# A decoder layer on one core: weight-block sums and the down products' sums into x made by accumulating transfers

## The chip, the cores and the metric

The kernel runs on one core of a Trainium2 chip. The metric is the device time of one execution in microseconds (us); lower is better. Three runs of the kernel before took 1016.21, 1017.39 and 1019.45 us.

The engines go by the names that the profile uses: PE multiplies matrices (PEld is its weight loading), DVE is the vector engine, ACT the scalar engine, POOL is GpSimd, SP issues most of the transfers. PSUM is the memory into which PE writes (8 banks); SBUF is the memory from which all engines read.

## What is computed

One layer of a decoder for 512 prompt tokens and 8 sample tokens (520 columns in all), with shared weights, and a final norm. What matters here is its last part, the feed-forward network:

```python
h2 = rms_norm(x, norm2_g) * (1.0 + sc2) + sh2
gu, up = jnp.split(h2 @ w_ffn_in, 2, axis=-1)
x = x + g2 * ((jax.nn.silu(gu) * up) @ w_ffn_out)
...
y = rms_norm(x, normf_g)
```

The model width is 1024, the inner width 2816, all in float32. Before it stand the input projections, a recurrent branch, attention over the prompt, attention of the 8 sample tokens over cached pages, and the projections that join them.

## The kernel before, in words

Activations lie transposed: `x` is eight tiles of 128 features by 520 columns. Every float32 operand is split into a high part and a low part of the matmul type (float32r); a product is three matmuls for each 128 rows of the inner dimension (high·high, low·high, high·low), with 260 columns at a time, half of the 520. The splits of weights are made just ahead of their use: ACT copies the source into the high half of a tile `wb`, and DVE subtracts that from the source to get the low half (`split_four`, L267 to L272). There are six `wb` buffers, so a split can run at most six units of weights ahead of PE.

The feed-forward part works through 22 tiles of 128 inner features. A tile needs two blocks of columns of `w_ffn_in` (gate and up), which SP loads with two transfers of 512 KB into one of two `wraw` buffers (`load_chunks`, L201). The tiles 0 to 3 are plain. The tiles 4 to 21 are made by `fast_tile` (L1658), which does the 2x2 block product with seven block products in place of eight (a scheme of Strassen and Winograd). The weight blocks are A11, A12 (gate, upper and lower half of the inner dimension) and A21, A22 (up), and four sums of them, S1 to S4. `split_block` (L255) makes the four sums on POOL, into two tiles `ws`, when the tile's first block is split: S1 = A21 + A22, S2 = S1 - A11, S3 = A11 - A21, S4 = A12 - S2. The matching sums of the activations are made once (`h2_blocks`, L1634). The seven products run in the order of `BLOCKS`: A11, S2, S3, S1, A12, A22, S4, 12 matmuls each, into four banks X, Y, W, Z; the banks are summed into each other between products (L1676 to L1692). Two orders matter below: the product A22 adds onto bank W, so it may start when DVE has made Y from W (L1685), and that needs ACT's copy of bank Z (L1683).

Between these products stand the down products, which multiply finished groups of four inner tiles with `w_ffn_out` (24 matmuls each, PE line L307, tile `fo`): in the tiles 4 to 16 one behind S2 and one behind A12, in 17 to 20 only the one behind A12, in 21 both. So 32 down products lie in the fast tiles. Each ends in `residual` (L1468), which adds gate times product into `x` with four DVE instructions: one multiply-add for the first half (L1470), and for the second half a small product of the 8 sample columns (L1475), a multiply-add (L1476) and a small sum (L1478). The last six inner tiles are multiplied at the end (`last_product`, L1563), which also does the final norm.

The order of each engine's queue is set by the program's order and a scheduler; each engine works its queue in order, and an instruction that waits holds everything behind it. SP's load of the tile c+2 waits until all that read the `wraw` buffer of tile c is done.

Of the kernel before, what the change touches and what calls it, by code (L numbers as in the profile page):

```python
# [8 lines left out]
F32 = mybir.dt.float32  # L9
F32R = mybir.dt.float32r  # L10
I32 = mybir.dt.int32
AF = mybir.ActivationFunctionType
ALU = mybir.AluOpType
# [5 lines left out]
NP = 512  # L19
# [5 lines left out]
KT = 8  # L25
# [3 lines left out]
HALF = NT // 2  # L29
HALVES = ((0, HALF), (HALF, NT))  # L30
# [35 lines left out]
def kernel(ctx, tc, xT, par, gates, b_f, cst, cse, own, cache_k, cache_v, cache_lf, pt,  # L66
# [3 lines left out]
    pe, act, dve, pool, sp = nc.tensor, nc.scalar, nc.vector, nc.gpsimd, nc.sync  # L70
# [4 lines left out]
    pgp = ctx.enter_context(tc.tile_pool(name="pgp", bufs=7))  # L75
# [4 lines left out]
    def slot(name, cols=NT, dt=F32, parts=128):  # L80
        return heap.tile([parts, cols], dt, name=name, tag="slot")
# [12 lines left out]
    x = []  # L94
# [19 lines left out]
    mod = keep.tile([128, 6, KT, 9], F32, name="mod")  # L114
# [25 lines left out]
    GROUP = 4  # L140
# [14 lines left out]

    for c in range(len(chunks)):
        whole(c)
    joined = set()
    for jt in range(FF // 128):
        c = len(chunks)  # L160
        chunks.append(cols(w_fi, 128 * jt, 128) + cols(w_fi, FF + 128 * jt, 128))
        if jt < GROUP:
            whole(c)
            continue
        for name in BLOCKS:
            units.append((c, name, 4))
            if name in JOIN[jt]:
                g, i = JOIN[jt][name]
                if i % 2 == 0:
                    joined.add(len(chunks))  # L170
                    chunks.append(cols(w_fo, 128 * i, 256, 128 * GROUP * g, GROUP))
                units.append((max(joined), 128 * (i % 2), GROUP))
# [7 lines left out]
    raws, splits = {}, {}  # L180
# [20 lines left out]
    def load_chunks(upto):  # L201
        while state["dma"] < len(chunks) and state["dma"] <= upto:
            c = state["dma"]
            if c in joined:
                raw = pgp.tile([128, GROUP, 256], F32, name="wraw", tag="pg")
            else:
                raw = wp.tile([128, KT, 256], F32, name="wraw", tag="wraw", bufs=2)
            o = 0
            for src, r0, nk, c0, n in chunks[c]:
                sp.dma_start(raw[:, :nk, o:o + n],  # L210
                             src[r0:r0 + nk * 128, c0:c0 + n].rearrange("(k p) c -> p k c", p=128))
                o += n
            raws[c] = raw
            state["dma"] += 1
# [7 lines left out]
    def split_upto(n):  # L222
        while state["split"] < len(units) and state["split"] <= n:
            m = state["split"]
            c, o, nk = units[m]
            load_chunks(c)
            raw = raws[c]
            state["split"] += 1
            if isinstance(o, str):
                splits[m] = split_block(raw, o)  # L230
                continue
            if c in joined:
                splits[m] = split_four(raw[:, :, o:o + 128])
                continue
            his, los = [], []
            step = 4 if m in in_heap else KT
            for k0 in range(0, nk, step):
                k1 = min(nk, k0 + step)
                if m in in_heap:
                    hi = slot("whs", 512, F32R).rearrange("p (k c) -> p k c", c=128)  # L240
                    lo = slot("wls", 512, F32R).rearrange("p (k c) -> p k c", c=128)
                else:
                    hi = wp.tile([128, KT, 128], F32R, name="whi", tag="whi", bufs=3)
                    lo = wp.tile([128, KT, 128], F32R, name="wlo", tag="wlo", bufs=3)
                src = raw[:, k0:k1, o:o + 128]
                state["act"] = act.copy(hi[:, :k1 - k0], src)  # L246
                with held(m):
                    state["last"] = dve.tensor_tensor(lo[:, :k1 - k0], src, hi[:, :k1 - k0].bitcast(F32), ALU.subtract)  # L248
                his += [hi[:, k] for k in range(k1 - k0)]
                los += [lo[:, k] for k in range(k1 - k0)]  # L250
            splits[m] = (his, los)

    blocks = {}

    def split_block(raw, name):  # L255
        if name == "A11":
            a11, a12, a21, a22 = (raw[:, k:k + 4, o:o + 128] for o in (0, 128) for k in (0, 4))
            s12, s34 = (pgp.tile([128, 8, 128], F32, name="ws", tag="pg") for _ in range(2))
            s1, s2, s3, s4 = s12[:, :4], s12[:, 4:], s34[:, :4], s34[:, 4:]
            blocks.update(A11=a11, A12=a12, A22=a22, S1=s1, S2=s2, S3=s3, S4=s4)  # L260
            pool.tensor_tensor(s1, a21, a22, ALU.add)  # L261
            pool.tensor_tensor(s2, s1, a11, ALU.subtract)
            pool.tensor_tensor(s3, a11, a21, ALU.subtract)
            pool.tensor_tensor(s4, a12, s2, ALU.subtract)
        return split_four(blocks[name])

    def split_four(src):  # L267
        state["tag"] = "wlo" if state.get("tag") == "whi" else "whi"
        t = wp.tile([128, KT, 128], F32R, name="wb", tag=state["tag"], bufs=3)
        state["act"] = act.copy(t[:, :4], src)  # L270
        state["last"] = dve.tensor_tensor(t[:, 4:], src, t[:, :4].bitcast(F32), ALU.subtract)  # L271
        return [t[:, k] for k in range(4)], [t[:, 4 + k] for k in range(4)]  # L272
# [49 lines left out]
    def product(name, a, evac, mid=None, inside=None):  # L322
        n = begin()
        for j in range(2):
            b = bank(f"{name}_{j}")
            half_product(n, j, a, b, None if j else inside)
            evac(j, b[:, :HALF])
            if j == 0 and mid is not None:
                mid()
        run_later(n)  # L330
# [1303 lines left out]
    def h2_blocks(k):  # L1634
        b1, b2 = h2raw[k], h2raw[k + 4]
        u, w = slot("u"), slot("w")
        with tc.issue_after(state["blocks"].ins) if k != 3 else nullcontext():
            first = pool.tensor_tensor(w[:, R_], b2[:, R_], b1[:, R_], ALU.subtract)
        if k == 3:
            state["blocks"] = first  # L1640
        with tc.issue_after(state["blocks"].ins):
            pool.tensor_tensor(u[:, L_], b1[:, R_], b1[:, L_], ALU.subtract)
            pool.tensor_tensor(w[:, L_], b2[:, R_], u[:, L_], ALU.subtract)
            pool.tensor_tensor(u[:, R_], b2[:, L_], w[:, L_], ALU.subtract)
        traw[k] = u, w

    def split_blocks(k0):
# [10 lines left out]
    def fast_tile(jt, ac):  # L1658
        sw, cp, u2, out = slot("sw"), slot("cp"), slot("u2", HALF), pair_out()
        X, Y, W, Z = (bank(f"fi{jt}{n}")[:, :HALF] for n in "xywz")  # L1660
        into = {"A11": X, "S2": Y, "S3": W, "S1": Z, "A12": X, "A22": W, "S4": Z}
        add = lambda o_, a_, b_: dve.tensor_tensor(o_, b_, a_, ALU.add)

        def close(b, part):
            dve.tensor_tensor(b, b, sw[:, part], ALU.mult)
            split_part(out, b, part)

        for m_, name in enumerate(BLOCKS):
            n = begin()
            hi, lo = splits[n]  # L1670
            for k in range(4):
                ah, al = h2_block(name, k)
                for m, (wt, at) in enumerate(((hi, ah), (lo, ah), (hi, al))):
                    state["mm"] = pe.matmul(into[name], lhsT=wt[k], rhs=at, start=m_ < 4 and k == 0 and m == 0,
                                            stop=k == 3 and m == 2, skip_group_check=m_ > 3)
            if name == "A11":  # L1676
                act.copy(cp[:, L_], X)
            elif name == "S2":
                add(u2, cp[:, L_], Y)
            elif name == "S3":  # L1680
                add(W, u2, W)
            elif name == "S1":
                act.copy(cp[:, R_], Z)  # L1683
                add(Z, u2, Z)
                add(Y, cp[:, R_], W)  # L1685
            elif name == "A12":
                act.activation(sw[:, L_], X, AF.Silu)
            elif name == "A22":
                close(W, L_)
            elif name == "S4":  # L1690
                act.activation(sw[:, R_], Z, AF.Silu)
                close(Y, R_)  # L1692
            run_later(n)
            if name in JOIN[jt]:
                g, i = JOIN[jt][name]
                product(f"fo{g}_{i}", ac[GROUP * g:GROUP * g + GROUP], lambda j, b_, i=i: residual(i, b_, 5, j))
        return out

    ac, ts, ready = [], [slot("sw") for _ in range(PLAIN)], []
    u = state["n"]  # L1700
    for j in range(2):
# [92 lines left out]
```

## Time and profile before

| | |
|---|---|
| runs | 1016.21, 1017.39, 1019.45 us; median 1017.39 |
| span of the profiled execution | 1016.4 us (1.0 below the median of the runs; its own time is recorded only as this span) |
| PE busy | 994.3 us, 98% of the span |
| DVE / ACT / POOL busy | 797.3 / 547.5 / 327.6 us |
| the fast tiles, 700 to 980 us | PE 280.00 of 280.00 us, DVE 233.91, ACT 133.05, POOL 97.04, granted clock 1.00, DMA share 0.34 |
| from 980 us to the end | PE 27.31 of 36.40 us |

How to read it: the columns of the windows view are stretch, length, busy time of each engine with its count of instructions, granted clock of PE, share of the DMA engines, GB/s. In the timeline a row is start, length, engine, line, operation, out<-in, and, in brackets, how long the engine stood idle before and what ended that. "us to landing" is the time from the start of a transfer's issue to the arrival of its last byte's signal.

### The profile page before, as it was taken

What the parts mean: (1) busy time and instruction counts of PE and PEld (TensorE: products, weight loads), DVE (VectorE), ACT (ScalarE), POOL (GpSimd) and SP (SyncE); (2) the same over time, 40 slices, a digit from 0 to 9 for tenths busy, and PEclk for the clock granted to TensorE, in tenths of its full rate; (3) what the DMA queues carried; (4) which work ended last, traced back from release to release, by engine and by line L of the source; (5) the groups of instructions that cost most, each with busy time, mean ns of one, the idle gap of its engine ahead of it and who ended that gap; (6) DMA issues with size and microseconds to landing.
All of it is one profiled execution on the core that took longest, in us unless ns stands there. A gap on an engine that the chain in (4) does not pass through costs nothing.

```text
span 1016.4 us, 21281 instructions
## 1 busy us (share of the span) xinstructions
PE 994.3 (98%) x8012; PEld 921.1 (91%) x8012; DVE 797.3 (78%) x1423; ACT 547.5 (54%) x1128; POOL 327.6 (32%) x415
## 2 busy tenths in 40 slices
PE   5999999999999999999999999999999999999996
PEld 2799999999998988888888888999999999999996
DVE  5559999998999888886655544869988888888764
ACT  4534576848761576777783233554444444445553
POOL 0346111121143245653400001583442442425112
PEclk9999999999999999999999999999999999999998
DMA  9798857788879998995867995324234243233122
GB/s 325 250 324 279 242 189 202 243 261 278 281 250 345 331 312 286 321 294 190 251 216 269 319 340 186 84 74 115 81 108 125 63 125 98 70 104 105 63 64 85
DMA packets 164378, 206.97 MB, mean 204 GB/s; under 512 B 9827, under 2 KB 125043, under 8 KB 164211
## 3 DMA queue, kind: packets, MB, share of 16 engines
q1 hardware_dynamic: 147634, 152.78, 48.1%
q0 software_dynamic: 12960, 46.41, 13.8%
q10 hardware_dynamic: 3680, 6.42, 1.7%
q8 instruction: 63, 1.03, 0.4%
q14 instruction: 41, 0.33, 0.1%
HBM read 192.49 MB, written 13.09 MB: 202 GB/s over the span
## 4 chain that ended last, share of the span: by engine, by line
PE 93%; DMA 2%; DVE 2%; ACT 1%; issue 0%; SPq 0%; POOL 0%; DVEq 0%; POOLq 0%; ACTq 0%
PE fo L307 12%; PE k L307 5%; PE wo L307 5%; PE gb L307 5%; PE gr L307 5%; PE v L307 5%; PE ga L307 5%; PE xr L307 5%; PE pb L307 4%; PE pv L839 3%; PE pa L307 3%; PE po L1302 2%; PE qp L542 2%; PE q L542 2%; PE ada L374 2%; PE ptt L1268 2%
## 5 line engine op out<-in xcount | busy, mean ns | idle before, releaser
L246 ACT CAST whi<-wraw 128x1024 fp32r<-128x1024 f32 (+1 forms) x79 | 82.0, 1039 | 113.6 <-PE pb L307 34.3
L248 DVE TENSOR_TENSOR wlo<-wraw,whi 128x1024 fp32r<-128x1024 f32 (+1 forms) x79 | 99.1, 1256 | 19.0 <-ACT whi L246 16.6
L307 PE MATMUL fo<-ach,wb 128*128 128x260 f32 x512 | 93.4, 283 | 0.0
L270 ACT CAST wb<-ws 128x512 fp32r<-128x512 f32 x72 | 44.7, 621 | 86.0 <-PE fo L307 58.9
L700 POOL DMA_DIRECT2D pg<-in_cache_k_dram x74 | 39.6, 536 | 143.1 <-DVE S L751 62.6
L271 DVE TENSOR_TENSOR wb<-wraw,wb 128x512 fp32r<-128x512 f32 x86 | 76.4, 889 | 4.7 <-ACT wb L270 3.9
L307 PEld LDWEIGHTS fo<-ach,wb 128*128 128x128 f32 x512 | 78.9, 188 | 0.0
L271 DVE TENSOR_TENSOR wb<-ws,wb 128x512 fp32r<-128x512 f32 x72 | 68.7, 954 | 12.6 <-ACT wb L270 11.0
L261 POOL TENSOR_TENSOR ws<-wraw 128x512 f32<-128x512 f32 x18 | 24.4, 1353 | 153.2 <-DMA wraw<-in_w_fi_dram 104.1
L307 PE MATMUL fo<-acl,wb 128*128 128x260 f32 x256 | 72.2, 282 | 0.0
L270 ACT CAST wb<-wraw 128x512 fp32r<-128x512 f32 x86 | 53.5, 622 | 31.4 <-ACT cp L1683 6.2
L750 DVE TENSOR_TENSOR pg<-pg,qb 128x1024 f32<-128x1024 f32 x48 | 57.9, 1221 | 2.5 <-DMA pg<-in_cache_k_dram 2.5
L751 DVE TENSOR_REDUCE S<-pg 128x16 f32<-128x1024 f32 x48 | 57.4, 1209 | 0.2
L1259 POOL TENSOR_SCALAR p<-p,mu 128x128 f32<-128x128 f32 (+3 forms) x28 | 38.4, 1381 | 53.0 <-DVE mu L1255 47.1
L307 PEld LDWEIGHTS fo<-acl,wb 128*128 128x128 f32 x256 | 48.2, 188 | 0.0
L1253 ACT ACTIVATE p<-p,mu 128x128 f32<-128x128 f32 (+3 forms) x64 | 35.4, 554 | 18.2 <-DVE mu L1252 18.0
L307 PE MATMUL v<-hh,whi 128*128 128x260 f32 x128 | 38.2, 298 | 0.8 <-ACT row L819 0.5
L307 PE MATMUL k<-hh,whi 128*128 128x260 f32 x128 | 37.3, 292 | 0.0
L307 PE MATMUL pb<-oh,whi 128*128 128x260 f32 x128 | 37.1, 290 | 0.2 <-ACT oh L1360 0.2
L307 PE MATMUL gb<-hh,whi 128*128 128x260 f32 x128 | 37.0, 289 | 0.0
L307 PE MATMUL v<-hl,whi 128*128 128x260 f32 x128 | 36.9, 288 | 0.0
L307 PE MATMUL v<-hh,wlo 128*128 128x260 f32 x128 | 36.9, 288 | 0.0
(1101 smaller groups left out, 3957.3 us busy)
## 6 DMA issues: line engine op xcount, KB each, us to landing
araw<-in_ada_w_dram SPq DMA_DIRECT2D x48, 512.0 KB, 7.6
wraw<-in_w_fi_dram SPq DMA_DIRECT2D x44, 512.0 KB, 5.3
pg<-in_cache_k_dram POOLq DMA_DIRECT2D x42, 512.0 KB, 6.2
pg<-in_cache_v_dram SPq DMA_DIRECT2D x42, 512.0 KB, 5.5
wraw<-in_w_in_dram SPq DMA_DIRECT2D x34, 512.0 KB, 6.4
wraw<-in_w_in_dram SPq DMA_DIRECT2D x11, 1024.0 KB, 8.5
pg<-in_cache_v_dram POOLq DMA_DIRECT2D x22, 512.0 KB, 6.1
pg<-in_cache_k_dram POOLq DMA_DIRECT2D x32, 256.0 KB, 5.9
```

What stands on the lines that cost most here:

```text
L246: state["act"] = act.copy(hi[:, :k1 - k0], src)
L248: state["last"] = dve.tensor_tensor(lo[:, :k1 - k0], src, hi[:, :k1 - k0].bitcast(F32), ALU.subtract)
L270: state["act"] = act.copy(t[:, :4], src)
L271: state["last"] = dve.tensor_tensor(t[:, 4:], src, t[:, :4].bitcast(F32), ALU.subtract)
L307: state["mm"] = pe.matmul(out[:, :t1 - t0], lhsT=wt[k], rhs=at, start=k == 0 and m == 0, stop=k == nk - 1 and m == 2)
L542: state["mm"] = pe.matmul(b[:, :HALF], lhsT=wt, rhs=at[:, t0:t1], start=k == 0 and m == 0, stop=k == 3 and m == 2)
L700: done.append(eng.dma_start(pg, cache[bass.ds(r, 1), :, c0:c1].rearrange("a p c -> (a p) c")))
L750: dve.tensor_tensor(pg, pg, q, ALU.mult)
L751: last = dve.tensor_reduce(S[r // 2][:, c:c + H], pg.rearrange("p (h d) -> p h d", d=DH), AX.X, ALU.add)
L839: pe.matmul(pv[0][32 * gq:32 * gq + 32, :], lhsT=pw[r][:, c:c + 32], rhs=pgs[gq // 2][:, 512 * hf:512 * hf + 512], start=j == 0, stop=j == ...
L1253: act.activation(p[:, :n + 128], p[:, :n + 128], AF.Exp, bias=mu[:, 0:1], scale=-1.0, accum_out=mu[:, 1:2])
L1259: (pool.tensor_scalar(p, p, mu[:, 2:3], None, ALU.mult) if a and i + 1 < KT else act.activation(p, p, AF.Copy, scale=mu[:, 2:3]))
```

## The change

- Of the four weight sums POOL still makes S1, and now S2 = S1 + A11. S3 is made in place: a transfer issued by POOL adds A11 onto A21 in the `wraw` buffer. S4 is also made in place: a second transfer adds S2 onto A12, when A12 itself has been split. The signs of the activations' sums and of two sums of banks are turned to match.
- The two halves of `wraw` now lie one behind the other, so that each block is one run of 2 KB in a partition.
- One tile `ws` a fast tile in place of two. `block_sums` of the next tile stands in the program behind the split of A12.
- A down product no longer goes to `residual`: ACT multiplies its two halves by the gate into a tile `dn`, DVE multiplies the 8 sample columns, and a transfer issued by POOL adds the 128x520 tile `dn` onto `x`.
- `load=28` lets the program's text reach further ahead with loads in this part.

```diff
+                if c in fast:
+                    raw = raw.rearrange("p k c -> p (k c)").rearrange("p (o k c) -> p o k c", o=2, k=KT)
...
-            pool.tensor_tensor(s1, a21, a22, ALU.add)
-            pool.tensor_tensor(s2, s1, a11, ALU.subtract)
-            pool.tensor_tensor(s3, a11, a21, ALU.subtract)
-            pool.tensor_tensor(s4, a12, s2, ALU.subtract)
-        return split_four(blocks[name])
+    def block_sums(c):
+        load_chunks(c)
+        raw = raws[c]
+        a11, a12, a21, a22 = (raw[:, o, k:k + 4] for o in range(2) for k in (0, 4))
+        s12 = pgp.tile([128, 8, 128], F32, name="ws", tag="pg")
+        s1, s2 = s12[:, :4], s12[:, 4:]
+        blocks[c] = dict(A11=a11, A12=a12, A22=a22, S1=s1, S2=s2, S3=a21, S4=a12)
+        pool.tensor_tensor(s1, a21, a22, ALU.add)
+        pool.dma_start(a21, a11, accum_op=ALU.add)
+        pool.tensor_tensor(s2, s1, a11, ALU.add)
+
+    def split_block(c, name):
+        if c not in blocks:
+            block_sums(c)
+        pair = split_four(blocks[c][name])
+        if name == "A12":
+            pool.dma_start(blocks[c]["S4"], blocks[c]["S2"], accum_op=ALU.add)
+            for d in sorted(fast):
+                if d > c:
+                    block_sums(d)
+                    break
+        return pair
...
-                product(f"fo{g}_{i}", ac[GROUP * g:GROUP * g + GROUP], lambda j, b_, i=i: residual(i, b_, 5, j))
+                product(f"fo{g}_{i}", ac[GROUP * g:GROUP * g + GROUP], lambda j, b_, i=i: add_down(i, b_, j))
...
+    def add_down(f, ps, j):
+        t0, t1 = HALVES[j]
+        e_, gate = min(t1, NP), mod[:, 5, f]
+        if j == 0:
+            downs[f] = slot("dn")
+        t = downs[f]
+        act.activation(t[:, t0:e_], ps[:, :e_ - t0], AF.Copy, scale=gate[:, 0:1])
+        if j:
+            dve.tensor_tensor(t[:, NP:], ps[:, e_ - t0:HALF], gate[:, 1:9], ALU.mult)
+            pool.dma_start(x[f], downs.pop(f), accum_op=ALU.add)
+
+    state.update(load=28)
```

The orders of PE and of SP are the same in both programs. Two places on other engines change. Lines of the changed program are higher (by 4 at the weight sums, by 14 around the fast tiles).

POOL's queue in the fast tiles before; `wraw_10599` and `wraw_10806` are the buffers of the tiles 7 and 8, `ws` their sums:

```order
L261 TENSOR_TENSOR ws_10735<-wraw_10599 128x512
L263 TENSOR_TENSOR ws_10736<-wraw_10599 128x512
L262 TENSOR_TENSOR ws_10735<-ws_10735,wraw_10599 128x512
L264 TENSOR_TENSOR ws_10736<-wraw_10599,ws_10735 128x512
L261 TENSOR_TENSOR ws_10942<-wraw_10806 128x512
L263 TENSOR_TENSOR ws_10943<-wraw_10806 128x512
L262 TENSOR_TENSOR ws_10942<-ws_10942,wraw_10806 128x512
L264 TENSOR_TENSOR ws_10943<-wraw_10806,ws_10942 128x512
```

The same place now; the buffers of the tiles 6, 7 and 8 are `wraw_10321`, `wraw_10527` and `wraw_10733`, and a row with DMA is a transfer that adds:

```order
L274 DMA wraw_10321<-ws_10451 128x512
L1724 DMA x_8824<-dn_10755 128x520
L265 TENSOR_TENSOR ws_10863<-wraw_10733 128x512
L266 DMA wraw_10733<-wraw_10733 128x512
L267 TENSOR_TENSOR ws_10863<-ws_10863,wraw_10733 128x512
L1724 DMA x_8826<-dn_10841 128x520
L274 DMA wraw_10527<-ws_10657 128x512
L1724 DMA x_8828<-dn_10961 128x520
```

Where four sums of one tile stood in a row, the S4 transfer of a tile (L274; tile 7 in the last row but one) now stands behind the sums of the tile after it (tile 8) and behind the sum into `x` of a down product of the tile before (`dn_10841`, tile 6).

ACT's queue around the split of S4 of tile 7 before (`ws_10736` holds S4, `wraw_10806` is tile 8):

```order
L1677 COPY cp_10899<-fi7x_10903 128x260
L270 CAST wb_10923<-wraw_10599 128x512
L270 CAST wb_10939<-ws_10736 128x512
L270 CAST wb_10948<-wraw_10806 128x512
L270 CAST wb_10982<-ws_10942 128x512
L1683 COPY cp_10899<-fi7z_10906 128x260
```

And now (`wb_10942<-wraw_10527` is the split of S4, which the transfer made in the `wraw` buffer of tile 7):

```order
L1691 COPY cp_10899<-fi7x_10903 128x260
L284 CAST wb_10923<-wraw_10527 128x512
L1721 ACTIVATE dn_10961<-fo0_6_0_10948,mod_102 128x260
L284 CAST wb_10942<-wraw_10527 128x512
L1721 ACTIVATE dn_10961<-fo0_6_1_10963,mod_102 128x252
L284 CAST wb_10945<-wraw_10733 128x512
L284 CAST wb_10979<-ws_10863 128x512
L1697 COPY cp_10899<-fi7z_10906 128x260
```

The split of S4 reads the `wraw` buffer, and the two halves of the down product behind S2 (`dn_10961`) stand around it.

More of the change, by code (lines that the diff above doesn't have):

```diff
@@ L157 @@
         whole(c)
-    joined = set()
+    joined, fast = set(), set()
     for jt in range(FF // 128):
@@ L164 @@
             continue
+        fast.add(c)
         for name in BLOCKS:
@@ L207, in load_chunks @@
                 raw = wp.tile([128, KT, 256], F32, name="wraw", tag="wraw", bufs=2)
+                if c in fast:
+                    raw = raw.rearrange("p k c -> p (k c)").rearrange("p (o k c) -> p o k c", o=2, k=KT)
             o = 0
             for src, r0, nk, c0, n in chunks[c]:
-                sp.dma_start(raw[:, :nk, o:o + n],
+                sp.dma_start(raw[:, o // 128] if c in fast else raw[:, :nk, o:o + n],
                              src[r0:r0 + nk * 128, c0:c0 + n].rearrange("(k p) c -> p k c", p=128))
@@ L229, in split_upto @@
             if isinstance(o, str):
-                splits[m] = split_block(raw, o)
+                splits[m] = split_block(c, o)
                 continue
@@ L253 @@
     blocks = {}
[L255 to L262, printed above, removed]
-            pool.tensor_tensor(s3, a11, a21, ALU.subtract)
-            pool.tensor_tensor(s4, a12, s2, ALU.subtract)
-        return split_four(blocks[name])
+    def block_sums(c):
[19 more added lines that the diff above has]
+        return pair
     def split_four(src):
@@ L1637, in h2_blocks @@
         with tc.issue_after(state["blocks"].ins) if k != 3 else nullcontext():
-            first = pool.tensor_tensor(w[:, R_], b2[:, R_], b1[:, R_], ALU.subtract)
+            first = pool.tensor_tensor(w[:, R_], b1[:, R_], b2[:, R_], ALU.subtract)
         if k == 3:
@@ L1641, in h2_blocks @@
         with tc.issue_after(state["blocks"].ins):
-            pool.tensor_tensor(u[:, L_], b1[:, R_], b1[:, L_], ALU.subtract)
-            pool.tensor_tensor(w[:, L_], b2[:, R_], u[:, L_], ALU.subtract)
-            pool.tensor_tensor(u[:, R_], b2[:, L_], w[:, L_], ALU.subtract)
+            pool.tensor_tensor(u[:, L_], b1[:, L_], b1[:, R_], ALU.subtract)
+            pool.tensor_tensor(w[:, L_], w[:, R_], b1[:, L_], ALU.subtract)
+            pool.tensor_tensor(u[:, R_], b2[:, L_], w[:, L_], ALU.add)
         traw[k] = u, w
@@ L1680, in fast_tile @@
             elif name == "S3":
-                add(W, u2, W)
+                dve.tensor_tensor(W, W, u2, ALU.subtract)
             elif name == "S1":
@@ L1684, in fast_tile @@
                 add(Z, u2, Z)
-                add(Y, cp[:, R_], W)
+                dve.tensor_tensor(Y, W, cp[:, R_], ALU.subtract)
             elif name == "A12":
@@ L1695, in fast_tile @@
                 g, i = JOIN[jt][name]
-                product(f"fo{g}_{i}", ac[GROUP * g:GROUP * g + GROUP], lambda j, b_, i=i: residual(i, b_, 5, j))
+                product(f"fo{g}_{i}", ac[GROUP * g:GROUP * g + GROUP], lambda j, b_, i=i: add_down(i, b_, j))
         return out
+    downs = {}
+    def add_down(f, ps, j):
[9 more added lines that the diff above has]
+    state.update(load=28)
     ac, ts, ready = [], [slot("sw") for _ in range(PLAIN)], []
```

## Prediction

> **What bounds the kernel now.** I read the page first, then the windows of the feed-forward part, PE's waits, and the timeline of one fast tile. The windows view of the fast tiles and of what follows them:
>
> ```profile
> span 1016.4 us, 21281 instructions
> 700.00:980.00 280.00, 280.00 (x2330) 279.86 (x2329) 233.91 (x445) 133.05 (x276) 97.04 (x66) 1.00 0.34 96
> 980.00:1016.40 36.40, 27.31 (x224) 26.44 (x223) 20.22 (x47) 16.60 (x36) 8.85 (x11) 0.93 0.19 62
> ```
>
> PE is busy for all of the 280 us, at the full granted clock. The waits view for PE from 690 us to the end has a single row:
>
> ```profile
> PE r L1593 <- ACT sq L1581: 0.2, 1, 0.2
> ```
>
> So in the part that the change touches PE waits for nothing; work taken from POOL or DVE there shortens nothing. The pace is read from the first matmul of neighbouring tiles (timeline, PE):
>
> ```profile
> 776.00 0.28 PE L1674 MATMUL fi9x<-h2h,wb 128*128 128x260 f32 x1
> 791.80 0.40 PE L1674 MATMUL fi10x<-h2h,wb 128*128 128x260 f32 x2
> 915.61 0.40 PE L1674 MATMUL fi18x<-h2h,wb 128*128 128x260 f32 x2
> 928.57 0.40 PE L1674 MATMUL fi19x<-h2h,wb 128*128 128x260 f32 x2
> ```
>
> A tile with two down products (132 matmuls) takes 15.80 us, one with a single down product (108) 12.96 us, both 0.12 us a matmul. From the first matmul of tile 4 to that of tile 21 there are 17 tiles: 13 long (4 to 16) and 4 short (17 to 20). Whatever must happen once a tile has to fit into these periods.
>
> **What is taken away.** The groups by line, 700 to 980 us (busy us, mean ns):
>
> ```profile
> L264 POOL TENSOR_TENSOR ws<-wraw,ws 128x512 f32<-128x512 f32 x16 | 26.3, 1646 | 1.3
> L262 POOL TENSOR_TENSOR ws<-ws,wraw 128x512 f32<-128x512 f32 x16 | 23.5, 1471 | 0.0
> L261 POOL TENSOR_TENSOR ws<-wraw 128x512 f32<-128x512 f32 x16 | 21.4, 1340 | 151.8 <-DMA wraw<-in_w_fi_dram 102.7 <-DVE wb L271 19.5 <-DVE fi11y L1662 10.0
> L1470 DVE SCALAR_TENSOR_TENSOR x<-fo,mod,x 128x260 f32<-128x260 f32 x32 | 15.5, 484 | 2.1 <-PE fo L307 1.2
> L1476 DVE SCALAR_TENSOR_TENSOR x<-fo,mod,x 128x252 f32<-128x252 f32 x32 | 15.1, 472 | 0.0
> L1478 DVE TENSOR_TENSOR x<-x,rs 128x8 f32<-128x8 f32 x32 | 12.3, 385 | 0.0
> ```
>
> DVE loses three of four instructions of each of 32 down products, 15.5 + 15.1 + 12.3 = 42.9 us. POOL loses two of four sums a tile, about 1.65 us each. ACT gains two scalings a down product; the nearest row is its Silu from PSUM:
>
> ```profile
> 786.84 0.38 ACT L1687 ACTIVATE sw<-fi9x 128x260 f32<-128x260 f32 x1
> ```
>
> 64 of these are 24 us on an engine that is busy for 133 of 280 us. None of this is on PE's path, so I cost all of it at nothing; if ACT's cover were gone, a tile would pay 1.5 us. The turned signs, the layout of `wraw` (the transfers read the same rows of the weights) and `load=28` (SP's order is unchanged) also cost nothing.
>
> **What is added: a ring around each tile.** Before, the load of tile c+2 waits for the split of A22 of tile c, and S3 and S4 lie elsewhere. The timeline around 780 us, and the load's issue by SP:
>
> ```profile
> 779.95 0.69 DVE L271 TENSOR_TENSOR wb<-wraw,wb 128x512 fp32r<-128x512 f32 x1
> 780.71 0.37 SPq L210 DMA_DIRECT2D wraw<-in_w_fi_dram  x1
> 786.68 1.29 POOL L261 TENSOR_TENSOR ws<-wraw 128x512 f32<-128x512 f32 x1 [9.79 <-DVE fi9z L1662]
> 782.01 0.62 ACT L270 CAST wb<-ws 128x512 fp32r<-128x512 f32 x1 [2.09 <-PE fo L307]
> 782.66 0.69 DVE L271 TENSOR_TENSOR wb<-ws,wb 128x512 fp32r<-128x512 f32 x1
> ```
>
> The buffer is free at 780.64, the load goes out at 780.71, POOL's first sum starts at 786.68. Nothing that POOL does then stands ahead of a load. In the changed program it does, because the last reader of the buffer is now the split of S4, and S4 comes from a transfer in POOL's queue behind the sums of the next tile. The ring: split of S4(c), load of c+2, S1, issue of the A21 transfer, S2, issue of a sum into `x`, S4(c+1) transfer, split of S4(c+1). Each step waits for the one before, and the ring must turn once a tile. POOL's issue of a transfer, and the landing times of its transfers, stand on the page and in the views of single issues at 87 and at 145 us:
>
> ```profile
> L700 POOL DMA_DIRECT2D pg<-in_cache_k_dram x74 | 39.6, 536 | 143.1 <-DVE S L751 62.6
> pg<-in_cache_k_dram POOLq DMA_DIRECT2D x32, 256.0 KB, 5.9
> pg<-in_cache_k_dram POOLq DMA_DIRECT2D x1, 256.0 KB, 3.0
> pg<-in_cache_k_dram POOLq DMA_DIRECT2D x1, 512.0 KB, 3.5
> q0 software_dynamic: 12960, 46.41, 13.8%
> ```
>
> No adding transfer is in this trace. S4's moves 256 KB, but an addition has two operands to read. The floor is the quiet plain transfer, 3.0 us; the ceiling the median of loads of this size beside full traffic, 5.9 us. I take the quiet 512 KB one, 3.5 us, since twice the data must pass, and the DMA engines are quiet here (share 0.34). The time on the DMA engines alone lies between twice the step from 256 to 512 KB (2 x 0.5 = 1.0 us) and POOL's queue mean (13.8% of 1016.4 us for 46.41 MB, 1.6 us for 512 KB); I take 1.3 us. The sum into `x` goes out one issue (0.54 us) ahead of S4 and so delays it by 1.3 - 0.54 = 0.8 us; S4 lands after 4.3 us.
>
> [...]
>
> The ring's length: handover to SP 0.07, load to first sum 786.68 - 780.71 = 5.97, S1 1.34, issue 0.54, S2 1.47, issue 0.54, S4 4.3, split 0.62 + 0.69 and handovers 0.1: 15.6 us. In a long tile the second half of the down product behind S2 is scaled by ACT behind the split of S4 (it stands there in ACT's queue), so its sum into `x` always goes out just as the next load starts, and takes 1.3 us of the DMA engines from it: 16.9 us.
>
> **The slack.** S4's lateness reaches PE by way of ACT: behind its split stand two splits of the next tile, then the copy of bank Z, and behind that on DVE the sums of Z and Y, for which the product A22 waits.
>
> ```profile
> 785.43 0.37 ACT L1683 COPY cp<-fi9z 128x260 f32<-128x260 f32 x1
> 788.93 0.28 PE L1674 MATMUL fi9w<-tuh,wb 128*128 128x260 f32 x1
> 783.39 0.44 DVE L1662 TENSOR_TENSOR fi9w<-fi9w,u 128x260 f32<-128x260 f32 x1
> ```
>
> From the start of S4's split to A22 on PE are 788.93 - 782.01 = 6.9 us. Back to back, the steps between take 0.62 on ACT, then on DVE three splits of 0.69 and three sums of about 0.44, 4.0 us, and the pieces of the down product some 0.2. That leaves 2.7 us, once.
>
> **The sum.** Long tiles: 13 x (16.9 - 15.8) = 14.3. Short ones: 4 x (15.6 - 12.96) = 10.6. Less the slack of 2.7: +22.2 us. The end is untouched: the last sums go into the features 6 and 7, which the final product reaches last, and what PE does not fill of the last 36 us is the norm, which the change leaves alone. The span becomes 1016.4 + 22.2 = 1038.6 us; the median of the runs, 1017.39, lies 1.0 above the span, so I say 1039.
>
> **The rivals.** *Hidden.* If S4's landing, with the queue ahead of it, stays under about 4 us, the long tiles fit. With plain prices (3.0 us, and 0.5 us for a sum into `x`, which goes out 0.54 ahead and is gone) the ring is 11.3 + 3.0 = 14.3, with the load's share 14.8, below 15.8; only the short tiles pay 4 x 1.4 - 2.7 = 2.8 us: 1020. For it: the DMA engines are two thirds idle. Against: two operands cannot cost less than one, and each further POOL wait adds. It ends at no change. *Costly.* S4 lands after 5.9 us, as loads of this size do at their median, and each sum into `x` takes 1.6: the ring is 17.2, with the load's share 18.8; 13 x 3.0 + 4 x 4.3 - 2.7 = +53: 1071. For it: the addition may run below the copying rate and the POOL issue may take longer than for a copy; against: 5.9 comes from a stretch of full traffic. *Faster.* It would need PE to run faster than 0.12 us a matmul when POOL and DVE read less. The same 0.12 holds for long and short tiles, and the only wait is 0.2 us. A matmul 1% quicker would give 2.8 us over 280: 1014. I give it 0.04.
>
> **How the numbers follow.** A change below 0.3% (3 us) is about what a measurement of this kernel can't tell from none. Forecast (a ring of 16 to 18 us in long tiles, slower) 0.50; costly 0.26, slower; hidden 0.20, of which 0.16 is within 0.3% and 0.04 beyond; faster 0.04. Slower 0.80, same 0.16, faster 0.04. The range goes from 1018, where most of the hidden case is taken in, to 1072, the costly case; beyond it lie the upper part of the costly case and the faster one.
>
> **What would show it.** Right: POOL's S1 starts a fast tile every 16 to 18 us; the split of S4 on ACT waits for a transfer `wraw<-ws`, some microseconds each tile; PE gets a wait of 1 us or more a tile, longest in the tiles 17 to 21; PE's busy time falls short of the span by some 20 us more. The landing of `wraw<-ws` gives the main term: 4.3 us by this sum, 3.0 if hidden, 6 or more if costly. Wrong: PE still without waits from 700 to 980 us, or its wait at banks that ACT has not emptied though S4 had landed in time, which would make ACT's added scalings, not the ring, the cause.

## The result, and the profile after

The changed kernel takes 1064.36 us (median of 4 runs, 1061.68 to 1066.64) beside 1017.68 us for the kernel before (4 runs, 1016.21 to 1019.45): a ratio of 1.0462, 95% interval 1.0445 to 1.0478. That is 46.7 us slower; the forecast was 22 us slower, and the range reached to 1072. So the direction and the place were right, and a size was not. The profiled execution has a span of 1061.2 us.

The window of the fast tiles in the changed kernel:

```profile
span 1061.2 us, 21428 instructions
700.00:980.00 280.00, 250.30 (x1981) 247.61 (x1980) 155.83 (x288) 127.91 (x287) 91.25 (x88) 0.95 0.60 138
```

PE was busy for 280.00 of these 280 us, and is now for 250.30 of them; the granted clock has gone from 1.00 to 0.95, and the share of the DMA engines from 0.34 to 0.60. PE's first matmuls of the tiles 4 and 21, before and after:

```profile
696.87 0.40 PE L1674 MATMUL fi4x<-h2h,wb 128*128 128x260 f32 x2
954.49 0.28 PE L1674 MATMUL fi21x<-h2h,wb 128*128 128x260 f32 x1
```

```profile
695.28 0.28 PE L1688 MATMUL fi4x<-h2h,wb 128*128 128x260 f32 x1
998.89 0.28 PE L1688 MATMUL fi21x<-h2h,wb 128*128 128x260 f32 x1
```

The same 17 tiles took 954.49 - 696.87 = 257.6 us and now take 303.6: 46.0 of the 46.7 us lie here. The waits of PE from 690 us on, where there was a single one of 0.2 us (total, times, longest):

```profile
PE fi6w L1688 <- DVE fi6y L1699: 5.0, 1, 5.0
PE fi17w L1688 <- DVE fi17y L1699: 4.4, 1, 4.4
PE fi19w L1688 <- DVE fi19y L1699: 4.2, 1, 4.2
PE fi13w L1688 <- DVE fi13y L1699: 3.2, 1, 3.2
```

All the long ones are at the product A22 (onto bank W), which waits for DVE's sum of bank Y, as the prediction had it. One turn of the ring, around 790 us. POOL's queue, then SP's load, then ACT (start, length):

```profile
786.21 1.28 POOL L265 TENSOR_TENSOR ws<-wraw 128x512 f32<-128x512 f32 x1 [6.28 <-DMA wraw<-in_w_fi_dram]
787.79 0.88 POOL L266 DMA_DIRECT2D wraw<-wraw  x1 [0.30 <-POOL ws L265]
788.38 1.60 POOL L267 TENSOR_TENSOR ws<-ws,wraw 128x512 f32<-128x512 f32 x1
789.61 1.21 POOL L1724 DMA_DIRECT2D x<-dn  x1
790.18 1.53 POOL L274 DMA_DIRECT2D wraw<-ws  x1
796.61 0.86 POOL L1724 DMA_DIRECT2D x<-dn  x1 [4.90 <-DVE dn L1723]
803.95 1.32 POOL L265 TENSOR_TENSOR ws<-wraw 128x512 f32<-128x512 f32 x1 [6.48 <-DMA wraw<-in_w_fi_dram]
...
796.31 0.99 SPq L213 DMA_DIRECT2D wraw<-in_w_fi_dram  x2
...
794.90 0.62 ACT L284 CAST wb<-wraw 128x512 fp32r<-128x512 f32 x1 [5.81 <-DMA wraw<-ws]
796.82 0.37 ACT L1697 COPY cp<-fi9z 128x260 f32<-128x260 f32 x1
```

The S4 transfer is issued at 790.18; ACT, which has waited for it for 5.81 us, splits S4 at 794.90; SP's load goes out at 796.31; POOL starts the first sum on what it brought at 803.95, 17.74 us after the first sum of the turn before (786.21). PE needs 15.8 us for such a tile. ACT's copy of bank Z (796.82) stands behind the split, and PE's product A22 behind that copy.

The landing times of these transfers, 700 to 1025 us (KB each, median us from issue to landing):

```profile
wraw<-in_w_fi_dram SPq DMA_DIRECT2D x32, 512.0 KB, 5.4
x<-dn POOLq DMA_DIRECT2D x32, 260.0 KB, 4.9
wraw<-ws POOLq DMA_DIRECT2D x17, 256.0 KB, 4.6
wraw<-wraw POOLq DMA_DIRECT2D x16, 256.0 KB, 3.3
```

The same 256 KB land in 3.3 us when nothing of POOL's goes ahead of them (`wraw<-wraw`), and in 4.6 us behind a sum into `x` (`wraw<-ws`).

### The profile page after: what moved, and what is told of

It is laid out like the page before. It is cut to its first block, busy times and chain, and to the rows that moved or that the text cites. A ratio compares the mean times of both kernels' runs of the same rounds, so it can differ in the third digit from the quotient of the medians.

```text
span 1061.2 us, 21428 instructions
## 1 busy us (share of the span) xinstructions
PE 1009.0 (95%) x8012; PEld 932.5 (88%) x8012; DVE 745.9 (70%) x1327; ACT 566.7 (53%) x1192; POOL 328.0 (31%) x447
## 4 chain that ended last, share of the span: by engine, by line
PE 65%; issue 14%; DMA 9%; POOL 5%; DVE 3%; ACT 3%; SPq 0%; ACTq 0%; DVEq 0%; POOLq 0%
DMA wraw<-ws 6%; PE wo L321 4%; PE gb L321 4%; PE pa L321 4%; PE gr L321 4%; PE ga L321 4%; PE xr L321 4%; PE pb L321 4%; PE fo L321 4%; PE k L321 4%; PE v L321 4%; PE pv L853 3%; POOL ws L265 2%; POOL x L1724 2%; PE qp L556 2%
## 5 line engine op out<-in xcount | busy, mean ns | idle before, releaser
L285 DVE TENSOR_TENSOR wb<-wraw,wb 128x512 fp32r<-128x512 f32 x122 | 109.0, 900 | 114.3 <-ACT wb L284 113.6
L284 ACT CAST wb<-wraw 128x512 fp32r<-128x512 f32 x122 | 75.2, 621 | 137.6 <-DMA wraw<-ws 94.1
L265 POOL TENSOR_TENSOR ws<-wraw 128x512 f32<-128x512 f32 x18 | 26.8, 1490 | 123.7 <-DMA wraw<-in_w_fi_dram 123.7
L1724 POOL DMA_DIRECT2D x<-dn x32 | 33.1, 1035 | 87.0 <-DVE dn L1723 87.0
L321 PE MATMUL xr<-hh,whi 128*128 128x260 f32 x128 | 36.7, 287 | 0.0
L321 PE MATMUL gr<-hh,whi 128*128 128x260 f32 x128 | 36.5, 285 | 0.0
L853 PE MATMUL pv<-pg,pw 128*32 128x512 f32 x256 | 36.2, 605 | 0.3 <-DMA pg<-in_cache_v_dram 0.3
```

The lines of the kernel that those rows point to most:

```text
L321: state["mm"] = pe.matmul(out[:, :t1 - t0], lhsT=wt[k], rhs=at, start=k == 0 and m == 0, stop=k == nk - 1 and m == 2)
L853: pe.matmul(pv[0][32 * gq:32 * gq + 32, :], lhsT=pw[r][:, c:c + 32], rhs=pgs[gq // 2][:, 512 * hf:512 * hf + 512], start=j == 0, stop=j == ...
L1724: pool.dma_start(x[f], downs.pop(f), accum_op=ALU.add)
```

## The experiments

The theory: the ring of the prediction (split of S4, load, S1, A21 transfer, S2, sum into `x`, S4 transfer) turns more slowly than PE, and nothing else costs time; only its length was put too low. The rivals: the added transfers cost by their amount, wherever they stand; ACT's scalings or the sums into `x` cost by themselves; PE's lower clock behind its waits adds to them.

**Cutting the ring by order alone.** S4's transfer stays ahead of the next tile's sums in POOL's queue:

```diff
-            pool.dma_start(blocks[c]["S4"], blocks[c]["S2"], accum_op=ALU.add)
+            s4 = pool.dma_start(blocks[c]["S4"], blocks[c]["S2"], accum_op=ALU.add)
...
-                    block_sums(d)
+                    with tc.issue_after(s4.ins):
+                        block_sums(d)
```

> All instructions and transfers of the changed kernel, but the S4 transfer of a tile is kept ahead of the next tile's weight sums in POOL's queue, so that S4(c+1) no longer waits for the load of tile c+2. Ring theory: the ring is cut, PE is full again in the fast tiles: 1018 us (1014 to 1026), no PE wait above 0.5 us there. Rival (the same transfers and scalings cost their time wherever they stand: contention on the DMA engines or ACT's added work): stays at 1055 to 1066.

Measured: 1017.58 us beside 1017.45, ratio 1.0003 (0.9989 to 1.0016). The window of the fast tiles and, from the landing times (700 to 960 us), the transfers of POOL in this kernel:

```profile
700.00:980.00 280.00, 280.00 (x2330) 279.85 (x2329) 206.63 (x344) 157.24 (x335) 103.86 (x102) 1.00 0.69 158
```

```profile
x<-dn POOLq DMA_DIRECT2D x30, 260.0 KB, 4.6
wraw<-ws POOLq DMA_DIRECT2D x18, 256.0 KB, 3.3
```

PE is full, and the DMA engines are busier (0.69) than in the slow kernel (0.60), since the same bytes pass in less time. All instructions and transfers of the change are there; the whole 46.7 us hang on whether S4's transfer stands ahead of the next tile's sums in POOL's queue or behind them.

**The same dose in both orders.** S2's sum is made twice, once in the changed kernel (first) and once in the reordered one (second):

```diff
         pool.tensor_tensor(s2, s1, a11, ALU.add)
+        pool.tensor_tensor(s2, s1, a11, ALU.add)
```

> The changed kernel with S2's sum made twice on POOL (the same result, 1.6 us more of POOL a tile), between the load and the next S4 transfer. Ring theory: every turn is longer by 1.6 us: 17 x 1.6 = 27 us over the changed kernel, 1091 (1082 to 1095). Rival (the added transfers' load on the DMA engines or PE sets the time, POOL is busy for a third only): 1062 to 1068.

> The same doubled sum in the kernel whose S4 transfer stands ahead of the next tile's sums. Ring theory: no ring, POOL has time, 1018 us (1014 to 1022). If a longer POOL chain costs time by itself, not by its place: 1035 to 1045.

Measured: 1088.74 us (ratio 1.0720, 1.0693 to 1.0747), 72.2 us above the kernel before where the changed kernel lies 46.7 above it, so 25.5 more, and 1017.18 us (1.0006, 0.9993 to 1.0019). 1.6 us of POOL in a tile cost 25.5 us inside the ring and nothing outside of it. POOL is busy for 92.81 of 250 us in the first and for 124.96 of 250 in the second, where PE is full:

```profile
700.00:950.00 250.00, 217.72 (x1672) 215.31 (x1672) 140.17 (x241) 107.18 (x241) 92.81 (x85) 0.93 0.57 130
```

```profile
700.00:950.00 250.00, 250.00 (x2087) 250.00 (x2086) 201.32 (x305) 141.07 (x301) 124.96 (x113) 1.00 0.71 162
```

**Each part alone.** First the sums into `x` alone (the kernel before with `add_down`), then S4 back on POOL with the other transfers kept:

```diff
-                product(..., lambda j, b_, i=i: residual(i, b_, 5, j))
+                product(..., lambda j, b_, i=i: add_down(i, b_, j))
```

```diff
+        s4 = pgp.tile([128, 8, 128], F32, name="ws", tag="pg")[:, :4]
...
+        pool.tensor_tensor(s4, a12, s2, ALU.add)
...
-            pool.dma_start(blocks[c]["S4"], blocks[c]["S2"], accum_op=ALU.add)
```

> The kernel before with one part of the change alone: the down products scaled by ACT and summed into x by transfers; the four weight sums on POOL as before. Ring theory: no transfer stands between the loads and the splits, so nothing turns in a ring: 1018 us (1014 to 1023), PE full. Rival (the transfers into x or ACT's scalings cost the time): 1030 to 1064.

> S4 is made by POOL in a second tile right behind S2, as before the change; S3 and the sums into x stay transfers. Ring theory: nothing waits for a transfer behind the next load, the buffer is free with the split of A12 and A22: 1018 us (1014 to 1023). Rival (S3's transfer or the sums into x cost by themselves): 1035 to 1064.

Measured: 1016.64 us (0.9998, 0.9989 to 1.0008) and 1017.72 us (1.0010, 1.0000 to 1.0019). PE is full from 700 to 980 us in both (the row is that of the first), and its only wait from 690 us on is the 0.2 us of before.

```profile
700.00:980.00 280.00, 280.00 (x2330) 279.85 (x2329) 191.68 (x349) 161.47 (x339) 123.66 (x97) 1.00 0.51 125
```

So the transfers into `x`, ACT's scalings and the S3 transfer cost nothing beyond the 2 us of these intervals without S4's. Next S3 back on POOL, S4 kept as a transfer:

```diff
-        pool.dma_start(a21, a11, accum_op=ALU.add)
+        pool.tensor_tensor(a21, a21, a11, ALU.add)
```

> One part of the change undone: S3 is made by POOL in place (a third sum of 1.3 to 1.6 us between S1 and S2) instead of by a transfer; S4 and the sums into x stay transfers, in the same order. Ring theory: from the start of S1 to that of S2 POOL takes 1.3 + 1.4 = 2.7 to 3.0 us instead of 1.91 + 0.59 = 2.50, so a turn gets longer by 0.2 to 0.5 us, or stays if S4's landing gains as much from the transfer left out: 17 turns, 1062 to 1074, though 4.3 MB fewer are moved. Rival (the amount moved by adding transfers sets the time): a third of the 48 transfers of weight sums and x in a tile's turn is gone, 1045 to 1055.

Measured: 1068.60 us (1.0502, 1.0478 to 1.0526). (The transfers left out are 18 of 68 in the fast tiles, a quarter, not the third that the expectation says.) Undoing this part gains nothing: the ring is no shorter (18.89 us a turn, in the table below), with a sum where the transfer's issue was. The landing of S4 gave back a little (4.3 us, from 4.6):

```profile
wraw<-ws POOLq DMA_DIRECT2D x17, 256.0 KB, 4.3
```

**Which terms of the ring were too small.** Three kernels take the sums into `x` out of the ring in different places. All down products by `residual` again, with S3 and S4 as transfers:

```diff
-                product(..., lambda j, b_, i=i: add_down(i, b_, j))
+                product(..., lambda j, b_, i=i: residual(i, b_, 5, j))
```

> The down products go by the four DVE instructions as before; the S3 and S4 transfers stay, and their order. Ring theory: no sum into x in POOL's queue: the wait for DVE's dn and the issue (1.24 and 0.58 us) shrink to one issue gap of 0.6, S4 lands in 3.3 us instead of 4.6, and the load is not disturbed (6.0 instead of 7.5 to first sum): turn 3.3 + 1.4 + 6.0 + 1.6 + 0.6 + 1.5 = 14.4 us. Long tiles (15.8) hide it, short ones pay 4 x 1.4: 1020 to 1024. Rival (S3 and S4 by transfer cost by themselves, the sums into x nothing): 1050 to 1066. A second rival, that the transfers into x and ACT's scalings alone cost the time, would also give 1018 to 1024 here and is told apart by the kernel that has them alone.

Measured: 1022.83 us (1.0063, 1.0041 to 1.0085).

Only the down product behind S2 by `residual`:

```diff
-                product(..., lambda j, b_, i=i: add_down(i, b_, j))
+                product(..., lambda j, b_, i=i: residual(i, b_, 5, j) if name == "S2" else add_down(i, b_, j))
```

> Of the two down products of a long tile the one behind S2 goes by the four DVE instructions again; the one behind A12 stays a transfer. So no transfer runs beside the load of a long tile. Ring theory with the mis-sized term in the load: the load's first sum comes after about 6.0 us instead of 7.6, the other terms stay: long turns 18.5 down to 16.9, 13 x 1.6 = 21 us less, about 1043 (1038 to 1050). Ring theory with the excess elsewhere (POOL's handovers, the landing): the load gives the 1.3 us that the forecast allowed, 17 us less, 1047, with the first sum at 6.3 us or later. Rival (the ring is not what sets the time): 1060 to 1066.

Measured: 1037.90 us (1.0207, 1.0183 to 1.0230), 21.3 us above the kernel before in place of 46.7, so 25.4 us less than the changed kernel, more than either expectation. By the table below the load gives 1.94 us of a turn; the rest is S1 to A21 (0.30) and S4's landing (0.23), which neither expectation had. One turn in POOL's queue; its load had gone out at 802.67, so the first sum on it starts after 808.36 - 802.67 = 5.69 us, where the changed kernel needed 803.95 - 796.31 = 7.64:

```profile
802.67 0.99 SPq L213 DMA_DIRECT2D wraw<-in_w_fi_dram  x2
...
808.36 1.29 POOL L265 TENSOR_TENSOR ws<-wraw 128x512 f32<-128x512 f32 x1 [10.29 <-DMA wraw<-in_w_fi_dram]
```

The sum into `x` behind A12 is held back until S4's transfer has gone out:

```diff
+            with tc.issue_after(s4.ins):
+                while waiting:
+                    f, t = waiting.pop(0)
+                    pool.dma_start(x[f], t, accum_op=ALU.add)
```

> The sum into x of the down product behind A12 is issued right behind the next S4 transfer instead of ahead of it; bytes and transfers are the same, the weight sums stay ahead of S4. Ring theory: the ring loses one issue (0.58 us) and the queue ahead of S4 (landing 4.6 down to about 3.3 us): 1.9 us a turn, long turns 18.5 down to 16.6, short 15.9 to 14.0: 13 x 0.8 + 4 x 1.0 = 14 us over before, 1032 (1022 to 1042). Rival (traffic or ACT): 1055 to 1066, since nothing is taken out.

Measured: 1037.85 us (1.0215, 1.0191 to 1.0239), 20.4 us above the kernel before, 26.3 us less than the changed kernel. S4 lands earlier, though the same transfers are issued:

```profile
wraw<-ws POOLq DMA_DIRECT2D x17, 256.0 KB, 3.7
x<-dn POOLq DMA_DIRECT2D x32, 260.0 KB, 5.8
```

The turns of these kernels side by side. The columns are means, in us, over the 13 turns from the S4 transfer of tile 4 to that of tile 17: S4's issue to its landing, landing to the load's issue, load to S1, S1 to the issue of the A21 transfer, from there to the next S4 issue, and the whole turn. The last columns hold the 17 turns from tile 4 to 21 less the 257.6 us of before, and what the kernel's time lies over that of the kernel before.

```
kernel                      landing  ->load  ->S1  ->A21  ->S4   turn | 17 turns  time
changed                        4.82    1.58  7.78   1.91  2.40  18.50 |    +46.4  +46.7
S2's down product residual     4.59    1.58  5.84   1.61  2.80  16.42 |    +20.1  +21.3
x behind S4                    3.75    1.58  7.91   1.95  1.82  17.01 |    +20.3  +20.4
all down products residual     3.42    1.58  6.39   1.69  2.76  15.85 |     +5.2   +5.4
S2 summed twice                4.63    1.52  7.67   1.83  4.38  20.02 |    +70.5  +72.2
S3 on POOL                                                      18.89 |    +51.2  +52.3
idle matmuls (below)           4.72    1.58  7.87   1.96  2.45  18.59 |    +48.2  +48.9
S4 ahead of the sums                                            15.73 |     +0.2   +0.1
```

In every kernel the lateness of the ring is the lateness of the kernel within 2 us. The load of the kernel without any sum into `x` (6.39) holds two turns of 7.9 and 8.6 us, for which no view gives a cause; its other eleven take 6.1 on average. (Where a turn is close to PE's 15.8, the step to S4 also holds a wait for PE's progress.)

**The lower clock.** The matmuls behind the longest waits come at a wider spacing. PE in tile 13 after its wait of 3.23 us, where three matmuls take 0.36 us at first (872.19 to 872.55) and then 0.65 us (872.94 to 873.59):

```profile
871.75 0.48 PE L1688 MATMUL fi13w<-tuh,wb 128*128 128x260 f32 x2 [3.23 <-DVE fi13y L1699]
...
872.19 0.40 PE L1688 MATMUL fi13w<-tuh,wb 128*128 128x260 f32 x2
872.43 0.29 PE L1688 MATMUL fi13w<-tul,wb 128*128 128x260 f32 x1
872.55 0.40 PE L1688 MATMUL fi13w<-tuh,wb 128*128 128x260 f32 x2
...
872.94 0.64 PE L1688 MATMUL fi13w<-tuh,wb 128*128 128x260 f32 x2
873.37 0.42 PE L1688 MATMUL fi13w<-tul,wb 128*128 128x260 f32 x1
873.59 0.64 PE L1688 MATMUL fi13z<-h2h,wb 128*128 128x260 f32 x2
...
876.59 0.41 PE L1688 MATMUL fi14x<-h2h,wb 128*128 128x260 f32 x2
```

Does that add to the time, or does it fill time in which PE would wait for the ring anyway? Matmuls whose result nothing reads keep PE busy ahead of A22:

```diff
+            if name == "A22":
+                for _ in range(16):
+                    pe.matmul(dump[:, HALF:HALF + 250], lhsT=h2[0][0][:, :128], rhs=h2[0][0][:, :250], start=True,
+                              stop=True, skip_group_check=True)
```

> The changed kernel plus 16 idle matmuls of 250 columns ahead of the product A22 in each of the 18 fast tiles, written into columns that nothing reads: about 1.9 us of PE a tile, 34 us in all, put where PE waits; the trace of the changed kernel has 32 us of waits there and matmuls at twice the spacing (granted clock 0.5) behind the longest ones, 13.5 us in all. Ring alone sets the time: PE's waits take the idle matmuls up, 1061 to 1068. Slow matmuls add to the time: PE stays busy and fast, 1050 to 1058. PE sets the time: 1080 to 1098.

Measured: 1066.38 us (1.0488, 1.0464 to 1.0513). PE is busy for 18.5 us more of this window and its clock is back at 1.00, but the time is that of the ring:

```profile
700.00:980.00 280.00, 268.83 (x2223) 266.31 (x2222) 156.53 (x286) 127.23 (x286) 92.40 (x88) 1.00 0.60 137
```

So neither the idle matmuls (an estimated 34 us: 16 in each of 18 tiles, at 0.12 us) nor the slow ones add anything beyond the 2.2 us by which this kernel lies above the changed one: both lie in time that the ring leaves to PE.

## Why the prediction was right in kind and too small in size

- **What is taken away is worth nothing:** right. With the sums into `x` alone, DVE is busy for 191.68 us of the window where it was for 233.91, 42.2 us less (42.9 by the forecast), and the time is that of before.
- **ACT's scalings, the signs, the layout, `load=28` cost nothing:** right, shown by the reordered kernel, which has them all.
- **The ring, and how it reaches PE:** right, by order, dose and table above.
- **The ring's length in a long tile, 16.9 us:** this is the step that failed. It is 18.50 us. By its terms:
  - *Load to the A21 transfer*, 9.69 in place of 5.97 + 1.3 + 1.34 = 8.61, is 1.1 too little. The share that the sum into `x` takes from the load was put at 1.3 us; it measures 7.78 - 5.84 = 1.9 beside the kernel with S2's down product by `residual`, 1.7 beside the three short turns of the changed kernel itself (6.05 on average, with no sum into `x` beside the load), and 1.4 beside the kernel without any (6.39). The A21 transfer waits another 0.3 us past the end of S1, which I had not counted. In two of the 13 turns its issue (713.20 and 734.30) comes 1.6 us after S1's end, for which no view names a wait: 0.2 us of the mean, and its cause stays open.
  - *S4's landing*, 4.82 in place of 4.3. Quiet, the transfer lands faster than I took (3.3 for 3.5). With no sum into `x` ahead but the A21 transfer issued 1.8 us before, it lands after 3.7 us ("x behind S4"), which is 0.4 us that I had not counted. The sum into `x`, issued 0.58 us ahead, makes that 4.6, so it delays S4 by 0.9 where I took 0.8. The other 0.2 us of the mean come from three turns (the transfers of the tiles 13, 14 and 16) that landed after 5.6 to 5.9 us; no run tells why.
  - *Split and handover*, 1.58 for 1.48, and *A21 to S4*, 2.40 for 2.55.

  Together that is +1.6 us, times 13 turns: 20.8 us.
- **The short tiles, 15.6 us:** three turns at 16.68 on average, +1.1 each. The last turn, from the S4 of tile 20 to that of tile 21 (1001.04), has no load in it any more and took 13.5 us; the forecast had 15.6 - 2.7 = 12.9 for a fourth short turn less the slack. Together +3.8 us. With the 20.8 this is 24.6, and 22.2 + 24.6 = 46.8 of the 46.7 measured.
- **The range's upper end** came from a plain transfer of 5.9 us, which S4's landing reached in three of 17 turns only. That the measured time lies within the range is owed to this bound and not to the sum; the loss came from smaller errors of the same sign, in transfers that meet. Their prices were worked out from plain transfers alone. An adding transfer lands nearly as fast (3.3 us, beside 3.0 for a plain one from DRAM), but one of 260 KB takes 1.4 to 1.9 us from the load, and an estimated 0.58 + 0.9 = 1.5 us from S4's transfer, where the step between plain ones of 256 and 512 KB was 0.5 us. What a plain one of that size would have cost in the same place was not measured.
- **The signs:** the split of S4 waits for `wraw<-ws`, and the waits of PE are where they were expected. They do not come once a tile, though, and are not longest in the tiles 17 to 21: the longest is 5.0 us in tile 6, and the tiles 4, 5, 7, 12 and 21 have none. No run tells why they come in clumps. PE's busy time (1009.0 us of 1061.2, after 994.3 of 1016.4) falls short of the span by 30 us more, not 20.
- **The rivals:** *hidden* failed by the same terms; in the kernel with all down products by `residual`, which has no sum into `x` in the ring, the turn of 15.85 us and the time of 1022.83 us are near its 1020. *Costly* came near in size by luck: S4 needed 4.82 us, not 5.9, and other terms made up for it. *Faster* has nothing for it: PE's 0.12 us a matmul is the same in all kernels where it is full.

A transfer that POOL issues takes from a load that SP issues: by the means of the table above the load brings its first sum after 7.78 us beside POOL's sum into `x`, and after 5.84 to 6.39 us without.

## What to carry to other kernels

When work goes from an engine to a transfer, draw the loop that runs through buffer reuse: what frees the buffer, what refills it, and what stands ahead of the transfer in its queue; if the loop comes back to itself once an iteration, its length, not any engine's load, is the new bound. Once that loop is longer than the pace of the engine that it feeds, every step in it counts in full, in every turn, so an error of 0.3 us in a term costs 5 us in 17 turns, and transfers that meet need a price for meeting, not only for running alone. A repair to try first is a queue order that opens the loop: here one constraint gave all 46.7 us back (though nothing beyond, since PE was full before).

## What the runs showed of the hardware

- Behind some waits PE's granted clock falls to half: the spacing of matmuls goes from 0.12 to 0.22 us for about 3.3 us (872.94 to about 876.2 in the rows above). In the changed kernel, from 690 us to 40 us before the end, the stretches at half clock begin at 743.15, 818.24, 872.85, 910.40, 944.53 and 978.67 us, whole multiples of 3.413 us apart, and last 3.41 or 6.83 us. They begin during or behind six of PE's waits: 4.99 us (tile 6), 1.97 (tile 10), 3.23 (tile 13), 2.77 (tile 15), 4.39 (tile 17) and 4.20 (tile 19); at the one of 1.90 us (tile 8) and the shorter ones there is none. Of the 3.41 us just ahead of each stretch PE was idle for 1.89 us (ahead of 818.24) to 3.41 us (ahead of 978.67). In the other windows of 3.413 us at full clock, counted on from these starts, it was idle for 1.45 us at the most (from 777.28, tile 8). Two rows around the wait of 1.97 us in tile 10 of the changed kernel, and two around the wait of 3.4 us in tile 17 of the kernel with S2's down product by `residual`, which lies partly in the one and partly in the other:

```profile
814.83:818.24 3.41, 1.52 (x13) 1.55 (x14) 3.01 (x7) 2.46 (x7) 0.68 (x1) 1.00 0.68 183
818.24:821.65 3.41, 3.41 (x18) 3.41 (x17) 1.47 (x3) 1.44 (x4) 0.00 (x0) 0.50 1.06 269
```

```profile
916.12:919.54 3.42, 1.69 (x15) 1.48 (x13) 1.34 (x3) 1.99 (x5) 0.00 (x0) 1.00 0.02 4
919.54:922.95 3.41, 1.78 (x14) 1.79 (x15) 2.86 (x8) 2.01 (x6) 0.00 (x0) 1.00 0.85 241
```

  PE was busy for 1.52 us of the first window, and the next ran at 0.50; in the second pair it was busy for 1.69 and 1.78 us, and the clock is 1.00 in both. No run of its own tests whether the place of a wait in these windows decides.
- 256 KB added from SBUF to SBUF by a transfer of POOL landed 3.3 us after the issue when no other transfer of POOL's went close ahead (`wraw<-wraw` of the changed kernel), and 3.7 us when one was issued 1.8 us before (`wraw<-ws` of "x behind S4"). In the turn around 790 us the row of an issue lasts 0.88 us with none close ahead (787.79), 1.21 us behind one issued 1.82 us before (789.61), and 1.53 us for the next one (790.18). POOL issued that next one 0.57 us after 789.61, within the row of 1.21 us.
- In the same turn the sum into `x`, which uses nothing of S2, is issued before S2 has ended (789.61, where S2 runs from 788.38 for 1.60 us); the A21 transfer, which overwrites what S1 reads, is issued 0.30 us past the end of S1 (787.79 after 787.49).
- DVE's splits from `wraw` take longer in the reordered kernel than those from `ws`, 1.08 beside 0.69 us on average (before, 0.88 and 0.95). The groups by line, 700 to 980 us:

```profile
L286 DVE TENSOR_TENSOR wb<-wraw,wb 128x512 fp32r<-128x512 f32 x118 | 126.4, 1078 | 48.3 <-ACT wb L285 47.4
L286 DVE TENSOR_TENSOR wb<-ws,wb 128x512 fp32r<-128x512 f32 x35 | 24.2, 691 | 16.3 <-ACT wb L285 16.3
```

  The traces show which are long: of the 152 splits that begin in this window, the 118 beside which POOL made no sum took 0.69 us at the most, and the 34 that ran for more than 0.05 us beside one took 2.05 us on average. In the kernel before it was 102 of 0.69 us at the most, and 52 of 1.35 on average. So the long splits go with a sum of POOL, and no wait in a view shows it. It costs nothing here, since DVE has 73 us to spare in this window.
